# Where the loads of norm factors, the first weight casts and the token sums stand in a two-layer trunk kernel

## The chip, the core and the metric

The kernel runs on one core of a Trainium2 chip. The metric is the time of one execution on the device in microseconds (us); lower is better. The core has engines that run side by side: PE (TensorE, matrix products and transposes), DVE (VectorE), ACT (ScalarE), POOL (GpSimd) and SP (SyncE, which here issues every transfer from and to DRAM). Each engine takes its instructions strictly in the order in which they were laid down when the program was built; an instruction that waits holds up all that stands behind it on the same engine.

## The reference

Two layers work on `h` of 512 tokens by 1024 channels, all float32. Each layer has four stages, and each stage begins with an RMS norm of `h` ("pre") and ends with an RMS norm of what it made ("post"), which is added to `h`:

```
h = h + 0.5 * rmsnorm(swiglu(rmsnorm(h, g[0]), ffn1_gu, ffn1_down), g[1])
z = rmsnorm(h, g[2]) @ w_in
mixed = concat(hgrn2(z), window_attention(z), spatial_gating(z)) @ w_out
h = h + rmsnorm(mixed, g[3])
h = h + 0.5 * rmsnorm(swiglu(rmsnorm(h, g[4]), ffn2_gu, ffn2_down), g[5])
gate = sigmoid(rmsnorm(h, g[6]) @ ple_gate)
h = h + rmsnorm((p @ ple_proj) * gate, g[7])
```

`swiglu(x)` is `(silu(x @ W_gate) * (x @ W_up)) @ W_down` with 2816 inner channels. `g` are the norm factors, eight rows of 1024 per layer.

## The kernel before, in words

Every large product is made of three matmuls on pairs "hi" and "lo": hi is a value rounded to the format that PE reads (a cast on ACT), lo is the rest (a subtraction on DVE, `split_lo`, L137). Weights come by DMA into a ring of two float32 buffers (`wst`), are cast (L156, L151, L280) and split (L137), and only then may PE use them; a load waits until the split has freed its buffer. The first weights of a stage go into buffers of their own, `uwh` and `uwl`.

The 512 tokens are four tiles of 128. At the end of a stage each tile t goes through a chain. `post_tile` (L173): ACT squares the two halves of the accumulator (`tmp`, L178), DVE adds the sums (`v`, L180) and multiplies by the norm factors (`tmp`, L181), POOL makes the inverse root (`r`, L162), DVE updates `h` (L185, two halves). `pre_tile` (L200) does the same for the next stage: squares on ACT (L204), `v` (L206), `r`, and the normed tile `hn` on DVE (L209). Then a "turn": PE transposes `hn` (`ptr`, L215, two times four), ACT casts the result to the hi part of `hT` (L218) and DVE subtracts the lo part (L219).

An ffn stage works on gate and up columns in 11 blocks of 256 columns. The first block is plain (`gu`, L238). The other ten are products of 2 x 2 blocks by Strassen's scheme with seven products instead of eight (M1 to M7, banks X, Y, Z, L361). For these the weights come in four quarters b11, b21, b12, b22 (`wraw`, L311), and differences of them are made on DVE (L321), cast (L316) and split. M1 needs b11, M2 b21, M5 (bank Z) b12 - b11, M6 (bank X again) b22 - b12 + b11. On the side of the tokens it needs four sums and differences S1 to S4 of four 512 x 256 quarters of `hT`: `token_sums` first adds hi and lo of each quarter (`A`, L292; two quarters on POOL, two on DVE), then combines them (L296), casts and splits. The finished `g` goes out to DRAM (`gd`), is read back for the down product (`acc`), and is cast and split there.

The mix stage begins with products for the spatial gate (`sg`) and goes on with `zf`, its recurrences, attention and `wo`. Its constants are loaded in `mix_params`, called in the middle of the ffn before it; the last step there is a matrix `wT`: PE transposes it (L629) and DVE multiplies it by a triangle (L631). The ple stage begins with `gate` and `pj` products.

The stages are generators. The main loop (L1177 to L1190) runs stage i to its end, starts stage i+1 up to its first `yield` (its first weights), and then makes the chains of the four tiles. A scheduler orders what each engine does, within what it is told: `tc.keep_in_program_order` (the code's `pin`) keeps an instruction behind the one pinned before on the same engine, `tc.issue_after(x)` keeps what is made within it behind x. On SP each load stands in one queue. The loads of norm factors (`gain`, `load_gain`, L166) are made in `ends()`, ahead of the down product, but not pinned, and stood in the queue at the end of the stage, among the first weights of the next.

Of the kernel before, what the change touches and what calls it, by code (L numbers as in the profile page):

```python
# [2 lines left out]

# [1 line left out]

# [67 lines left out]
def kernel(ctx: ExitStack, tc: tile.TileContext, a: dict, out: bass.AP, phases=None):  # L73
# [59 lines left out]

    WST = 2

    def split_lo(out_, in_, hi, eng=nc.vector):
        eng.tensor_tensor(out=out_, in0=in_, in1=hi.bitcast(F32), op=ALU.subtract)  # L137

    def w_pair():
        return tuple(wpool.tile([P, 1024], F32R, tag=x, name=x) for x in ("whi", "wlo"))  # L140
# [1 line left out]
    def load_w(view, k=None, utag=None, eng=nc.vector):  # L142
        st = wpool.tile([P, 1024], F32, tag="wst", name="wst", bufs=WST)
        nc.sync.dma_start(st[:].rearrange("p (a b) -> p a b", a=k) if k else st[:], view)
        if utag and PHASE[cur["kind"]][utag][1] == 1024:
            hi, lo = ut("uwh", utag, F32R), ut("uwl", utag, F32R)
        elif utag:
            his = [ut("uwh", utag, F32R) for _ in range(2)]
            los = [ut("uwl", utag, F32R) for _ in range(2)]
            for n in range(2):  # L150
                nc.scalar.copy(his[n][:], st[:, n * 512:(n + 1) * 512])  # L151
# [4 lines left out]
        nc.scalar.copy(hi[:], st[:])  # L156
        split_lo(lo[:], st[:], hi[:], eng)
        return lambda c, w=512: (hi[:, c:c + w], lo[:, c:c + w])

# [6 lines left out]
    def load_gain(l, i):  # L166
        g = []
        for n in range(2):
            g.append(bpool.tile([P, 512], F32, tag="gain", name=f"gain{l}{i}{n}", bufs=4))
            nc.sync.dma_start(g[n][:], a["norm_gains"][l, i:i + 1, HN[n]].to_broadcast([P, 512]))  # L170
        return g

    def post_tile(t, parts, g, scale):  # L173
# [89 lines left out]
    def ffn(l, w_gu, w_down, i, ends, hook):  # L263
# [4 lines left out]
        def four(x):  # L268
            return x[:].rearrange("p (a b) -> p a b", a=4)
# [5 lines left out]
        for gu in range(2):  # L275
            for q in range(2):
# [4 lines left out]
                split_lo(lo[:], st[:], hi[:], nc.gpsimd if gu == q == 0 and i == 0 else nc.vector)  # L281
                w[gu, q] = hi, lo
        yield
        hT = hTs[i]
        turn(0)
        turn(1)

        def token_sums():
            def whole(half, q, tag, eng):
                x = ut("A32", "z") if tag == "z" else wpool.tile([P, 1024], F32, tag=tag, name="A32", bufs=WST)  # L290
                hi, lo = (hT[1][y][:, :, HALVES[half]].bitcast(F32) for y in (q, 2 + q))
                eng.tensor_tensor(out=four(x), in0=hi, in1=lo, op=ALU.add)  # L292
                return x

            def make(n, x, y, op, out):
                nc.vector.tensor_tensor(out=out[:], in0=x[:], in1=y[:], op=op)  # L296
                nc.scalar.copy(S[n][0][:], out[:])
                split_lo(S[n][1][:], out[:], S[n][0][:])

            a11, a12 = (whole(0, q, "z", nc.gpsimd) for q in range(2))  # L300
            a21, a22 = (whole(1, q, "wst", nc.vector) for q in range(2))
            make(1, a21, a22, ALU.add, a22)
            make(3, a11, a21, ALU.subtract, a21)
            make(2, a22, a11, ALU.subtract, a11)
            make(4, a12, a11, ALU.subtract, a12)


# [65 lines left out]
        def prefetch(n=1):  # L373
            for _ in range(n):
                x = next(ahead, None)
                if x:
                    queue.append(x)

        for tok in HALVES:
            for m in range(2):  # L380
                for gu in range(2):
# [101 lines left out]
    def ple(l, i, ends):  # L483
# [7 lines left out]
        for k in range(2):  # L491
# [147 lines left out]
    def mix_body(l, i_, ends, prms):  # L639
# [530 lines left out]
    pre(1, "pm")  # L1170
    run = phase(0)
    next(run)
    load_x(2)
# [40 lines left out]
```

## Time and profile before

| | us |
|---|---|
| median of 3 runs | 2044.76 (2043.82 to 2045.81) |
| the profiled execution, its own time | 2045.54 |
| its span in the profile | 2043.8 |
| PE busy | 1961.9 |
| DVE busy | 1405.4 |
| ACT busy | 926.7 |
| POOL busy | 135.2 |

Times in the profile count from the start of the span. A row of the timeline has start, duration, engine, line, operation, output and inputs, shape and count, and in brackets the idle time before it with what ended it. Rows of the view by windows have the window, its length, PE busy time (instructions), the clock granted to PE as a share of full speed, the share of DMA time and GB/s.

### The profile page before, as it was taken

The numbers are of one execution on the slowest core, as the hardware profiler recorded it, in microseconds if no ns is written. First come the engines' busy times: TensorE is split into PE (matmuls) and PEld (weight loads), VectorE is DVE, ScalarE is ACT, GpSimd is POOL, SyncE is SP. The second block draws the span as 40 slices with busy tenths as digits, with TensorE's granted clock in tenths as the row PEclk, the third lists the DMA queues.
The fourth block names the chain that finished last, engine by engine and source line by source line (L and its number), as shares of the span: only waits on it lengthen the run. The fifth ranks groups of instructions, "written<-read, shape, count | busy, mean of one in ns | idle before, by whom it ended". The sixth has DMA issues, their size and how long they took to land.

```text
span 2043.8 us, 31112 instructions
## 1 busy us (share of the span) xinstructions
PE 1961.9 (96%) x12524; PEld 1759.5 (86%) x12524; DVE 1405.4 (69%) x2054; ACT 926.7 (45%) x1467; POOL 135.2 (7%) x143
## 2 busy tenths in 40 slices
PE   6999999999989999998989999999999899999988
PEld 6999988788769999887789999887877799998866
DVE  7888663679769888434688785347798687874354
ACT  4544442554545445323454553335545455453242
POOL 2000000113110000000110000001130100000000
PEclk9999999999999999999999999999999999999999
DMA  6534263423225342542254433535141254335421
GB/s 195 175 120 140 85 206 120 147 60 116 77 67 168 115 147 84 177 146 90 72 170 126 149 112 111 176 114 151 56 129 42 73 165 155 109 99 185 144 95 50
DMA packets 160033, 251.18 MB, mean 123 GB/s; under 512 B 11408, under 2 KB 116752, under 8 KB 159888
## 3 DMA queue, kind: packets, MB, share of 16 engines
q1 hardware_dynamic: 159888, 249.19, 38.2%
q8 instruction: 98, 1.61, 0.3%
q14 instruction: 47, 0.39, 0.1%
HBM read 217.17 MB, written 29.36 MB: 121 GB/s over the span
## 4 chain that ended last, share of the span: by engine, by line
PE 79%; DVE 11%; DMA 4%; ACT 3%; issue 2%; POOL 1%; SPq 0%; DVEq 0%; POOLq 0%; ACTq 0%
PE X L361 22%; PE Z L361 11%; PE acc L235 8%; PE acc L234 8%; PE acc L233 8%; PE Y L361 5%; DVE wlo L137 2%; DMA wst<-in_ffn_gate_up_dram 2%; PE gate L234 1%; PE gate L235 1%; DMA wraw<-in_ffn_gate_up_dram 1%; PE gate L233 1%; PE gu L238 1%; DVE Pm L973 1%; DVE hn L209 1%
## 5 line engine op out<-in xcount | busy, mean ns | idle before, releaser
L316 ACT CAST whi<-wraw 128x1024 fp32r<-128x1024 f32 x280 | 291.9, 1050 | 363.1 <-DVE wraw L321 138.5
L137 DVE TENSOR_TENSOR wlo<-wraw,whi 128x1024 fp32r<-128x1024 f32 x280 | 340.4, 1221 | 101.1 <-ACT whi L316 100.3
L137 DVE TENSOR_TENSOR wlo<-wst,whi 128x1024 fp32r<-128x1024 f32 x148 | 185.2, 1251 | 153.6 <-ACT whi L156 152.5
L234 PE MATMUL acc<-wlo,gh 128*128 128x512 f32 x704 | 274.3, 390 | 0.1
L233 PE MATMUL acc<-whi,gh 128*128 128x512 f32 x704 | 274.2, 389 | 0.0
L235 PE MATMUL acc<-whi,gl 128*128 128x512 f32 x704 | 273.4, 390 | 0.0
L156 ACT CAST whi<-wst 128x1024 fp32r<-128x1024 f32 x140 | 147.1, 1051 | 206.2 <-PE acc L235 83.3
L361 PE MATMUL X<-hT,whi 128*128 128x256 f32 x1280 | 232.7, 283 | 3.1 <-DVE c L435 3.1
L321 DVE TENSOR_TENSOR wraw<-wraw 128x1024 f32<-128x1024 f32 x160 | 194.9, 1222 | 14.7 <-DMA wraw<-in_ffn_gate_up_dram 11.2
L361 PEld LDWEIGHTS X<-hT,whi 128*128 128x128 f32 x1280 | 199.6, 192 | 3.9 <-DVE c L435 3.9
L361 PE MATMUL X<-hT,wlo 128*128 128x256 f32 x640 | 181.1, 283 | 0.0
L235 PEld LDWEIGHTS acc<-whi,gl 128*128 128x128 f32 x704 | 132.1, 188 | 29.0 <-DVE gl L468 1.6
L234 PEld LDWEIGHTS acc<-wlo,gh 128*128 128x128 f32 x704 | 132.2, 188 | 28.5 <-DVE wlo L137 1.2
L233 PEld LDWEIGHTS acc<-whi,gh 128*128 128x128 f32 x704 | 132.2, 188 | 27.0
L162 POOL TENSOR_TENSOR r<-v,mhalf 128x1 f32<-128x1 f32 x64 | 38.1, 595 | 1715.4 <-DVE v L180 1608.6
L468 DVE TENSOR_TENSOR gl<-gl,gh 128x1024 fp32r<-128x1024 f32 x44 | 53.9, 1224 | 102.2 <-ACT gh L467 102.0
L361 PEld LDWEIGHTS X<-hT,wlo 128*128 128x128 f32 x640 | 122.8, 192 | 0.0
L361 PE MATMUL Y<-hT,whi 128*128 128x256 f32 x640 | 116.9, 283 | 0.0
L361 PEld LDWEIGHTS Y<-hT,whi 128*128 128x128 f32 x640 | 99.8, 192 | 0.0
L467 ACT CAST gh<-gl 128x1024 fp32r<-128x1024 f32 x44 | 46.3, 1053 | 110.4 <-PE acc L234 105.2
L361 PE MATMUL X<-S2h,wlo 128*128 128x256 f32 x320 | 91.5, 286 | 4.0 <-DVE wlo L137 4.0
L361 PE MATMUL X<-S2h,whi 128*128 128x256 f32 x320 | 91.2, 285 | 0.4 <-ACT whi L316 0.4
(326 smaller groups left out, 4694.9 us busy)
## 6 DMA issues: line engine op xcount, KB each, us to landing
wraw<-in_ffn_gate_up_dram SPq DMA_DIRECT2D x160, 512.0 KB, 5.4
wst<-in_ffn_down_dram SPq DMA_DIRECT2D x88, 512.0 KB, 3.4
gd<-g SPq DMA_DIRECT2D x44, 512.0 KB, 6.2
gl<-gd SPq DMA_DIRECT2D x44, 512.0 KB, 3.4
wst<-in_w_in_dram SPq DMA_DIRECT2D x36, 512.0 KB, 3.8
gain<-in_norm_gains_dram SPq DMA_DIRECT2D x32, 256.0 KB, 4.7
wst<-in_ffn_gate_up_dram SPq DMA_DIRECT2D x16, 512.0 KB, 6.5
wst<-in_w_out_dram SPq DMA_DIRECT2D x16, 512.0 KB, 3.4
```

The lines of the kernel that those rows point to most:

```text
L137: eng.tensor_tensor(out=out_, in0=in_, in1=hi.bitcast(F32), op=ALU.subtract)
L156: nc.scalar.copy(hi[:], st[:])
L162: nc.gpsimd.tensor_tensor(out=r, in0=v, in1=mhalf[:, :w], op=ALU.pow)
L209: nc.vector.scalar_tensor_tensor(out=hn[n][:], in0=h[t][n][:], scalar=r, in1=g[n][:], op0=ALU.mult, op1=ALU.mult)
L233: pin(nc.tensor.matmul(acc, lh, rh, start=first, stop=False))
L234: pin(nc.tensor.matmul(acc, lh, rl, start=False, stop=False))
L235: pin(nc.tensor.matmul(acc, ll, rh, start=False, stop=last))
L316: nc.scalar.copy(hi[:], x[:])
L321: nc.vector.tensor_tensor(out=out[:], in0=x[:], in1=y[:], op=ALU.subtract)
L361: pin(nc.tensor.matmul(acc[:, m * 256:(m + 1) * 256], x[:, c], y, start=fresh and m == k == n == 0, stop=m == 1 and k == 3 and n == 2, ski ...
L467: nc.scalar.copy(gh[:], gl[:].bitcast(F32))
L468: nc.vector.tensor_tensor(out=gl[:], in0=gl[:].bitcast(F32), in1=gh[:].bitcast(F32), op=ALU.subtract)
```

## The change

Three edits:

1. `load_gain` pins its DMAs, which puts the loads of norm factors on SP where the code stands: at the beginning of the down product, or behind the last loads of the output weights in mix, and no longer among the next stage's first weights.
2. `mix` and `ple` yield twice, each time with the newest hi cast and lo split. The main loop wraps the chain of tile 0 in `issue_after` of the first pair and its turn in that of the second. So the first weights of the stage (two of mix, four of ple) are cast and split ahead of tile 0's norms, and more of them ahead of tile 0's turn. The ffn yields twice with nothing, so there the wrapping is empty.
3. In `token_sums` all four sums of hi and lo are on DVE, pinned; the order is two sums, S1, one sum, S3, S2, one sum, S4. `prefetch(1)`, which loads b11 and b21 of the second block and casts the weight of M1, stands ahead of the token loop instead of within it.

```
 def load_gain(l, i):
-            nc.sync.dma_start(g[n][:], a["norm_gains"][l, i:i + 1, HN[n]].to_broadcast([P, 512]))
+            tc.keep_in_program_order(nc.sync.dma_start(g[n][:], a["norm_gains"][l, i:i + 1, HN[n]].to_broadcast([P, 512])))
...
+    @contextmanager
+    def behind(marks):
+        with ExitStack() as st:
+            for x in marks or ():
+                st.enter_context(tc.issue_after(x.ins))
+            yield
+
+    def marks():
+        return newest["hi"], newest["lo"]
...
 def token_sums():
-                eng.tensor_tensor(out=four(x), in0=hi, in1=lo, op=ALU.add)
+                pin(nc.vector.tensor_tensor(out=four(x), in0=hi, in1=lo, op=ALU.add))
...
-            a11, a12 = (whole(0, q, "z", nc.gpsimd) for q in range(2))
-            a21, a22 = (whole(1, q, "wst", nc.vector) for q in range(2))
+            a21, a22 = (whole(1, q, "wst") for q in range(2))
             make(1, a21, a22, ALU.add, a22)
+            a11 = whole(0, 0, "z")
             make(3, a11, a21, ALU.subtract, a21)
             make(2, a22, a11, ALU.subtract, a11)
+            a12 = whole(0, 1, "z")
             make(4, a12, a11, ALU.subtract, a12)
...
+        prefetch(1)
         for tok in HALVES:
...
-                prefetch(1)
                 token_sums()
                 prefetch(2)
...
 def ple(l, i, ends):
-        wg = [load_w(a["ple_gate"][l, k * P:(k + 1) * P, :], utag="bcc"[k] if k < 3 else None) for k in range(KD)]
-        yield
+        wg = []
+        for k in range(KD):
+            wg.append(load_w(a["ple_gate"][l, k * P:(k + 1) * P, :], utag="bcc"[k] if k < 3 else None))
+            if k in (1, 3):
+                yield marks()
...
 def mix_body(l, i_, ends, prms):
-        w = rows_cols(1792, 2)
-        yield
+        w = []
+        for j in range(4):
+            w.append(load_w(W[j * 256:(j + 1) * 256, 1792:].rearrange("(k p) c -> p k c", p=P), 2, "e" if j < 2 else None))
+            if j in (1, 2):
+                yield marks()
...
-            next(run)
+            ahead = next(run)
         for t, parts, g, scale, npre in todo:
-            post_tile(t, parts, g, scale)
-            turns[t] = npre(t, later=True)
+            with behind(ahead if t == 0 else None):
+                post_tile(t, parts, g, scale)
+                turns[t] = npre(t, later=True)
...
+            if t == todo[0][0] and i + 1 < len(seq):
+                ahead = next(run)
             if t < 2:
-                turn(t)
+                with behind(ahead if t == 0 else None):
+                    turn(t)
```

How the change moves instructions shows in three places. The first is DVE where the first ffn ends and mix begins, in layer 0. `tmp` and `h_80`, `h_81` are tile 0's post norm, `hn` its pre norm, `wT` the matrix of the spatial gate. Before:

```order
L181 SCALAR_TENSOR_TENSOR tmp_3628<-acc00_2766,gain010_2746 128x512
L631 TENSOR_TENSOR wT_3004<-wT_2999,triu_2997 128x512
L180 TENSOR_SCALAR v_3630<-ssq_3627 128x1
L181 SCALAR_TENSOR_TENSOR tmp_3629<-acc01_2767,gain011_2748 128x512
L185 SCALAR_TENSOR_TENSOR h_80<-tmp_3628,r_3636,h_80 128x512
L185 SCALAR_TENSOR_TENSOR h_81<-tmp_3629,r_3636,h_81 128x512
```

And now:

```order
L197 SCALAR_TENSOR_TENSOR tmp_3616<-acc00_2766,gain010_2746 128x512
L196 TENSOR_SCALAR v_3618<-ssq_3615 128x1
L197 SCALAR_TENSOR_TENSOR tmp_3617<-acc01_2767,gain011_2748 128x512
L201 SCALAR_TENSOR_TENSOR h_80<-tmp_3616,r_3624,h_80 128x512
L652 TENSOR_TENSOR wT_3004<-wT_2999,triu_2997 128x512
L201 SCALAR_TENSOR_TENSOR h_81<-tmp_3617,r_3624,h_81 128x512
L139 TENSOR_TENSOR wlo_3644<-wst_3641,whi_3643 128x1024
L222 TENSOR_SCALAR v_3635<-ss_3630 128x1
L225 SCALAR_TENSOR_TENSOR hn_3631<-h_80,r_3637,gain020_2750 128x512
L225 SCALAR_TENSOR_TENSOR hn_3632<-h_81,r_3637,gain021_2752 128x512
```

The multiplication of `wT` has moved from ahead of tile 0's update of `h` to between its two halves. On PE the four transposes that it waits for have moved too, from within the last accumulations to behind all of them.

The second place is ACT where the second ffn ends and ple begins, in layer 0: `uwh` are the first weights of ple, `tmp` the squares of tile 0's post norm, `hT30` the hi part of its transposed tile. Before:

```order
L156 CAST uwh_9172<-wst_9170 128x1024
L218 CAST hT30_8439<-ptr_9276 128x512
L156 CAST uwh_9178<-wst_9176 128x1024
L218 CAST hT30_8439<-ptr_9283 128x512
L178 ACTIVATE tmp_9292,ssq_9290<-acc11_8446 128x512
L156 CAST uwh_9206<-wst_9204 128x1024
```

And now:

```order
L142 CAST uwh_9172<-wst_9170 128x1024
L142 CAST uwh_9178<-wst_9176 128x1024
L142 CAST uwh_9206<-wst_9204 128x1024
L142 CAST uwh_9212<-wst_9210 128x1024
L194 ACTIVATE tmp_9217,ssq_9216<-acc00_8443 128x512
L194 ACTIVATE tmp_9218,ssq_9216<-acc01_8444 128x512
L142 CAST uwh_9242<-wst_9240 128x1024
L220 ACTIVATE hn_9230,ss_9229<-h_5194 128x512
L220 ACTIVATE hn_9231,ss_9229<-h_5195 128x512
L142 CAST whi_9248<-wst_9246 128x1024
```

Four casts have moved ahead of tile 0's squares, and two more ahead of its `hT`.

The third place is the queue of SP where the second ffn of layer 0 begins. `wst` are weights of the first block, `wraw_6066` is b12 of the second block and `wraw_6072` its b22, `wraw_6308` to `wraw_6374` are the quarters of the third block. Before:

```order
L278 DMA wst_5876<-in_ffn2_gate_up_dram 128x4x256
L278 DMA wst_5882<-in_ffn2_gate_up_dram 128x4x256
L311 DMA wraw_6066<-in_ffn2_gate_up_dram 128x4x256
L170 DMA gain051_8433<-in_norm_gains_dram 128x512
L170 DMA gain060_8435<-in_norm_gains_dram 128x512
L170 DMA gain061_8437<-in_norm_gains_dram 128x512
L311 DMA wraw_6308<-in_ffn2_gate_up_dram 128x4x256
L311 DMA wraw_6310<-in_ffn2_gate_up_dram 128x4x256
L311 DMA wraw_6343<-in_ffn2_gate_up_dram 128x4x256
L311 DMA wraw_6072<-in_ffn2_gate_up_dram 128x4x256
```

And now:

```order
L294 DMA wst_5876<-in_ffn2_gate_up_dram 128x4x256
L294 DMA wst_5882<-in_ffn2_gate_up_dram 128x4x256
L329 DMA wraw_6308<-in_ffn2_gate_up_dram 128x4x256
L329 DMA wraw_6310<-in_ffn2_gate_up_dram 128x4x256
L329 DMA wraw_6343<-in_ffn2_gate_up_dram 128x4x256
L329 DMA wraw_6374<-in_ffn2_gate_up_dram 128x4x256
L329 DMA wraw_6066<-in_ffn2_gate_up_dram 128x4x256
L416 DMA gd0_5912<-g_6045 128x1024
L329 DMA wraw_6072<-in_ffn2_gate_up_dram 128x4x256
```

The gain loads have left the queue here. b12 has moved from the first loads to behind the third block's four quarters, and b22 to behind the store of the first block's `g`.

More of the change, by code (lines that the diff above doesn't have):

```diff
@@ L1 @@
 import math
-from contextlib import ExitStack
+from contextlib import ExitStack, contextmanager
 import numpy as np
@@ L134, with cast_hi @@
     WST = 2
+    newest = {}
     def split_lo(out_, in_, hi, eng=nc.vector):
-        eng.tensor_tensor(out=out_, in0=in_, in1=hi.bitcast(F32), op=ALU.subtract)
+        newest["lo"] = eng.tensor_tensor(out=out_, in0=in_, in1=hi.bitcast(F32), op=ALU.subtract)
+    def cast_hi(out_, in_):
+        newest["hi"] = nc.scalar.copy(out_, in_)
+    @contextmanager
[6 more added lines that the diff above has]
+        return newest["hi"], newest["lo"]
     def w_pair():
@@ L150, in load_w @@
             for n in range(2):
-                nc.scalar.copy(his[n][:], st[:, n * 512:(n + 1) * 512])
+                cast_hi(his[n][:], st[:, n * 512:(n + 1) * 512])
                 split_lo(los[n][:], st[:, n * 512:(n + 1) * 512], his[n][:], eng)
@@ L155, in load_w @@
             hi, lo = w_pair()
-        nc.scalar.copy(hi[:], st[:])
+        cast_hi(hi[:], st[:])
         split_lo(lo[:], st[:], hi[:], eng)
@@ L283, in ffn @@
         yield
+        yield
         hT = hTs[i]
@@ L288, in token_sums, with whole @@
         def token_sums():
-            def whole(half, q, tag, eng):
+            def whole(half, q, tag):
                 x = ut("A32", "z") if tag == "z" else wpool.tile([P, 1024], F32, tag=tag, name="A32", bufs=WST)
                 hi, lo = (hT[1][y][:, :, HALVES[half]].bitcast(F32) for y in (q, 2 + q))
-                eng.tensor_tensor(out=four(x), in0=hi, in1=lo, op=ALU.add)
+                pin(nc.vector.tensor_tensor(out=four(x), in0=hi, in1=lo, op=ALU.add))
                 return x
@@ L1172 @@
     next(run)
+    next(run)
     load_x(2)
```

## The prediction

> **What bounds the kernel now.** The page's first part says that the matmul engine works nearly all the time:
>
> ```profile
> PE 1961.9 (96%) x12524; PEld 1759.5 (86%) x12524; DVE 1405.4 (69%) x2054; ACT 926.7 (45%) x1467; POOL 135.2 (7%) x143
> ```
>
> So the edit can win or lose only where PE stands still. The list of waits of PE (engine, line, what it waited for: us in total, times, longest) names the places:
>
> ```profile
> PE ptr L215 <- DVE hn L209: 32.0, 14, 7.8
> PE gate L233 <- ACT uwh L156: 6.4, 2, 3.2
> PE X L361 <- DVE wlo L137: 4.0, 3, 1.8
> PE gate L234 <- DVE uwl L137: 4.0, 2, 2.1
> ```
>
> `ptr` are the transposes of normed tokens, waiting for norms at a stage's end; `gate` waits for the first weights of ple; `X` for a split weight difference in an ffn. The counts of two are the two layers, and the edit reorders both layers alike, so I work the first out and count it twice.
>
> A wait costs more than itself. The view by windows (busy us of PE, granted clock) shows it on the chip's own 3.41 us grid:
>
> ```profile
> 384.39:387.80 3.41, 1.48 (x7) 1.00 0.80 219
> 387.80:391.21 3.41, 3.07 (x7) 0.50 0.82 275
> 585.78:589.19 3.41, 0.16 (x1) 1.00 0.00 0
> 589.19:592.60 3.41, 2.33 (x10) 0.50 0.00 0
> 592.60:596.02 3.42, 3.42 (x10) 0.50 0.00 0
> 957.83:961.24 3.41, 1.36 (x2) 0.50 0.40 154
> 961.24:964.66 3.42, 3.37 (x9) 0.50 0.47 153
> ```
>
> A window with PE busy for 1.48 or 0.16 us is followed by one at half clock, in which a full 3.41 us of work advances 1.7. So a wait of about 2 us costs 1.7 more, one of 4 us up to 3.4 more. [...]
>
> **Entry of mix (ffn1 to mix): a loss.** Before, the `wT` transposes stood early in the last accumulations and VectorE's multiplication of `wT` was done at 353.4; the norms of tile 0 followed and PE found them ready at 370.23:
>
> ```profile
> 353.38 0.69 DVE L631 TENSOR_TENSOR wT<-wT,triu 128x512 f32<-128x512 f32 x1 [0.75 <-PE wT L629]
> 355.67 1.42 DVE L185 SCALAR_TENSOR_TENSOR h<-tmp,r,h 128x512 f32<-128x512 f32 x2
> 358.82 1.41 DVE L209 SCALAR_TENSOR_TENSOR hn<-h,r,gain 128x512 f32<-128x512 f32 x2 [0.73 <-POOL r L162]
> 370.23 1.04 PE L215 MATMUL ptr<-ident,hn 128*128 128x128 f32 x8
> 388.14 0.80 PE L233 MATMUL sg<-uwh,hT 128*128 128x512 f32 x1 [2.28 <-ACT hT L218]
> 401.47 0.39 PE L233 MATMUL zf<-hT,whi 128*128 128x512 f32 x1
> ```
>
> Now `wT` is transposed behind the last accumulation, and its multiplication stands on VectorE between tile 0's two updates of `h`. So everything behind it (the second `h`, the squares, the norms of all four tiles) waits until about 370.2 (acc ends half of a 1.04 row earlier, four transposes follow). From there: the multiplication 0.7, then from the second `h` to the first `hn` as long as before, 356.4 to 359.5, about 3.2. With 0.2 of latency `ptr` starts near 374.4, a wait of 4.2. Behind it the norms of tiles 2 and 3, which used to be spread, come in a row on VectorE: I count 0.75 before the low half of tile 0, 0.8 in tile 1, and 2.4 around tile 2, whose low `hT` stands behind the updates of tile 3; 4.0 together. One half-clock window (1.7) follows. That is 9.9. Before, the same stretch lost 2.8 in waits, 2.28 of them the one that makes the window 384.39 idle, and 1.7 at half clock, 4.5. The casts moved ahead gain little here: before, PE began its `sg` matmuls 0.24 us after the transposes anyway. **+5.4 less 0.2 for cover of the half clock by those waits: +5.2.** Bounds: +3.5 (no half window), +8 (two, as after the wait at 590.27 below, and a longer tile 2).
>
> **Entry of ple (ffn2 to ple): a gain.** Before:
>
> ```profile
> 941.95 1.04 ACT L156 CAST uwh<-wst 128x1024 fp32r<-128x1024 f32 x1
> 954.88 1.05 ACT L156 CAST uwh<-wst 128x1024 fp32r<-128x1024 f32 x1
> 953.76 1.04 PE L215 MATMUL ptr<-ident,hn 128*128 128x128 f32 x8
> 957.99 1.36 PE L233 MATMUL gate<-uwh,hT 128*128 128x512 f32 x2 [3.19 <-ACT uwh L156]
> 961.24 0.80 PE L234 MATMUL gate<-uwl,hT 128*128 128x512 f32 x1 [1.89 <-DVE uwl L137]
> 983.80 0.63 PE L215 MATMUL ptr<-ident,hn 128*128 128x128 f32 x4 [0.37 <-DVE hn L209]
> ```
>
> ScalarE cast one weight at 941.95 and the next only at 954.88, behind a cast of `hT` that waited for PE's transposes, so 12 us of ScalarE went unused, and PE stood still for 3.19, 1.89, 0.42 and 0.37 (5.9) and ran the two windows from 957.83 at half clock (3.4). Now four weights are cast before tile 0's norms and two more before its `hT`. The norms come later (four casts and splits of 1.05 and 1.2 plus two loads in their way: 941.7 instead of 936), but are ready near 949, still ahead of 953.76: cover of 5 us. What is late next are the splits of the fifth and sixth weight, behind tile 1's updates: 0.7 and 0.75, with 0.7 of smaller waits, 2.2, and no window is idle for long. So 5.9 and 3.4 go and 2.2 comes: **−7.1.** Bounds −5 and −8.5.
>
> **Entry of ffn2 (mix to ffn2): a gain.** GpSimd sums tokens exactly while VectorE does the step that PE waits for:
>
> ```profile
> 587.30 3.48 DVE L209 SCALAR_TENSOR_TENSOR hn<-h,r,gain 128x512 f32<-128x512 f32 x2 [0.73 <-POOL r L162]
> 590.27 1.94 PE L215 MATMUL ptr<-ident,hn 128*128 128x128 f32 x8 [4.33 <-DVE hn L209]
> 603.28 3.45 POOL L292 TENSOR_TENSOR A<-hT,hT 128x1024 f32<-128x1024 f32 x1
> 604.39 3.55 DVE L185 SCALAR_TENSOR_TENSOR h<-tmp,r,h 128x512 f32<-128x512 f32 x2
> 610.48 0.66 PE L215 MATMUL ptr<-ident,hn 128*128 128x128 f32 x4 [2.16 <-DVE hn L209]
> ```
>
> Alone these steps take 1.41 and 1.42 (rows at 358.82 and 355.67); beside a sum 3.48 and 3.55. Without the sums the waits shrink by 2.07 and 2.06, one of the two half windows from 589.19 goes (1.7), and 0.4 for weights whose load no longer stands behind gain loads: **−6.2.** Bounds −4 and −8. The gain loads by themselves are worth that 0.4. At their new place, the start of the down product, they stand ahead of the third slice's weights, as three constant loads did in the first ffn:
>
> ```profile
> 249.43 0.40 PE L233 MATMUL acc<-whi,gh 128*128 128x512 f32 x1
> 249.66 0.40 PE L234 MATMUL acc<-wlo,gh 128*128 128x512 f32 x1
> 258.16 1.05 ACT L156 CAST whi<-wst 128x1024 fp32r<-128x1024 f32 x1 [6.25 <-DMA wst<-in_ffn_down_dram]
> ```
>
> The down product starts at 249.43 and takes 24 matmuls of 0.23 us a slice, so the third slice is due near 260.4: cover of 1 us behind its cast, and a cost of nothing while it holds; without it, four loads at 0.4 us of issue each, 1.6 per ffn.
>
> **Second block of every ffn (M5, M6): a loss.** The sums now cost VectorE two more 1.2 us steps, and the third weight quarter (b12) is loaded behind the four quarters of the next block, the fourth (b22) behind the store of `g`. Before:
>
> ```profile
> 625.20 4.82 SPq L311 DMA_DIRECT2D wraw<-in_ffn_gate_up_dram  x5
> 634.88 3.50 DVE L321 TENSOR_TENSOR wraw<-wraw 128x1024 f32<-128x1024 f32 x3 [2.61 <-DMA wraw<-in_ffn_gate_up_dram]
> 635.09 0.28 PE L361 MATMUL Z<-S1h,whi 128*128 128x256 f32 x1
> 639.56 0.38 PE L361 MATMUL X<-S2h,wlo 128*128 128x256 f32 x1 [1.20 <-DVE wlo L137]
> ```
>
> The five loads are freed by PE's reads, as now, so the fifth lands about when the fourth did here, 634.9. Then on VectorE: the difference b12−b11, S4's low part, c11, the low part of the difference: 1.2, 1.1, 0.6, 1.2, so M5 (`Z`) runs from 638.8 instead of 635.09. Its 24 matmuls take 3.0; b22's differences and split (two, a cast, a split) end at 643.6, where `X` went on at 639.56: +4.0, and 0.3 left of a half window that the second wait mostly covers. Per ffn: **ffn2 +4.3 in both layers; ffn1 of layer 0, which had no wait there, +4.2; ffn1 of layer 1, +3.2,** since it already lost 1.77 at half clock:
>
> ```profile
> 1067.60 0.58 PE L361 MATMUL X<-S2h,wlo 128*128 128x256 f32 x1 [1.77 <-DVE wlo L137]
> ```
>
> Bounds per ffn: +2 (b12 in the queue's shortest landing) to +7 (two half windows, later landing).
>
> **Entry of the two ffn1.** The same contention, smaller:
>
> ```profile
> 23.09 0.63 PE L215 MATMUL ptr<-ident,hn 128*128 128x128 f32 x4 [1.99 <-DVE hn L209]
> 27.07 0.63 PE L215 MATMUL ptr<-ident,hn 128*128 128x128 f32 x4 [2.04 <-DVE hn L209]
> 1037.87 0.52 PE L215 MATMUL ptr<-ident,hn 128*128 128x128 f32 x3 [2.58 <-DVE hn L209]
> ```
>
> In layer 0 4.0 of waits shrink to 1.3 (the fourth weight, landing at 23.7, is next): −2.7. In layer 1, 2.58 loses the 2.1 of a stretched step: −2.1.
>
> **Sum**, against the profiled execution's 2045.54 us: mix 2 × 5.2 = +10.4; ple 2 × −7.1 = −14.2; ffn2 entries 2 × −6.2 = −12.4; M5/M6 4.3 + 4.3 + 4.2 + 3.2 = +16.0; ffn1 entries −4.8. Total −5.0: 2040.5. The median of the runs shown is 0.8 below the profiled time, so 2040 as a median. About 0.2%, 4.1 us, is what a measurement of this kernel can tell from no change.
>
> **Rivals.**
> - *M5 and M6 cost 7 each (slower).* Place: the low part of b12's difference on VectorE, which waits for a load in the middle of a shared queue. If two windows at half clock follow instead of one partly covered (as at 589.19), or b12 lands 2 us later, each ffn loses 2.8 more: 4 × 2.8 = +11, 2052. It turns the total from 2.3 per ffn on. For it: the row at 589.19. Against: PE runs matmuls, not transposes, right behind the wait. Chance 0.20.
> - *Mix loses 8 each.* Two half windows behind a 4 us wait, as at 589.19 and 592.60; total −5.0 + 5.6, 2046. Chance 0.24.
> - *b12 is not late.* If its load lands at 632 and VectorE has slack before it, M5 and M6 lose 1 each: −17, 2028.5. For: 2.61 us of VectorE idle stood there. Against: the two sums fill that. Chance 0.13.
> - [...] Chance 0.05. [...]
>
> Forecast 0.38. That the edit does not do what it says is excluded by the order of instructions, which is fixed before the run. Faster by over 0.2%: 0.30 of the forecast (it lies near the bound), 0.13, 0.05, so 0.48; within: 0.08 and 0.20 of the mix case, 0.28; slower: 0.20 and 0.04, 0.24. The range 2028 to 2053 takes in the b12 case and the slow case.
>
> **What would show it.** Right: `ptr` behind a wait near 4 us at the entry of mix; no wait over 1 us in ple before its 48 gate matmuls of tile 1; `h` and `hn` at 1.4 everywhere and no GpSimd sum; `Z` of the second block behind a 3 to 4 us wait, then `X` behind one over 1. Wrong: no wait at `Z`, or the mix stage starting its `zf` at the same distance from the last `acc` as before, 31.2 us.

## The result and the profile after

| | before | after |
|---|---|---|
| median of 4 runs, us | 2044.29 (2043.15 to 2045.81) | 2056.25 (2055.23 to 2056.91) |
| profiled execution, its own time | 2045.54 | 2056.59 |
| its span | 2043.8 | 2054.8 |

The ratio is 1.0058, with a 95% interval from 1.004 to 1.0075: slower by 12 us, where 2040 had been forecast and 2053 was the end of the range. No work was added for PE. The page's first part of the changed kernel, and its list of waits of PE (engine, line, what it waited for: us in total, times, longest):

```profile
PE 1969.0 (96%) x12524; PEld 1765.8 (86%) x12524; DVE 1398.7 (68%) x2062; ACT 925.7 (45%) x1467; POOL 113.2 (6%) x135
```

```profile
PE ptr L231 <- DVE hn L225: 26.7, 14, 8.3
PE Z L379 <- ACT whi L334: 12.0, 4, 3.8
PE Z L379 <- DVE wlo L139: 7.7, 4, 4.2
PE acc L249 <- ACT whi L142: 4.7, 4, 1.4
```

The waits of `gate` have left the list, those of `ptr` are shorter, and two groups are new: `Z`, the first product that needs b12, four times twice, and `acc`, in the down products. To find where the time went I mark the start of each stage in both traces and compare the lengths of the stretches between them. The sum of the stretches is the difference of the spans (11.0) but for 0.4 before the first and behind the last mark.

| stretch, us after less before | forecast | ffn1, layer 0 / 1 | ffn2, layer 0 / 1 |
|---|---|---|---|
| entry of ffn1 (to the first X) | −2.7 / −2.1 | −2.1 / −1.6 | |
| entry of ffn2 (`wo` to the first X) | −6.2 each | | −4.1 / −7.3 |
| second block (first X to the third block's Y) | +4.2 / +3.2; +4.3 each | +8.4 / +4.4 | +5.8 / +5.9 |
| down product | 0 | +1.9 / +1.0 | +1.4 / +1.2 |
| entry of mix (behind ffn1) | +5.2 each | +5.8 / +4.7 | |
| ple (behind ffn2) | −7.1 each | | −7.2 / −7.6 |

Mix and ple came out as forecast, and the entries of the ffns within 2.1 in sum. The second blocks lost 24.5 instead of 16.0, and the down products 5.5 instead of nothing. Those 14.0 are all but 1.6 of the 15.6 between the forecast sum and the traces.

**Second block.** In layer 0's ffn2 (timeline of PE: start, us, engine, line, operation, and in brackets the idle time before it with what ended it):

```profile
644.90 0.28 PE L379 MATMUL Y<-hT,wlo 128*128 128x256 f32 x1
648.28 0.39 PE L379 MATMUL Z<-S1h,whi 128*128 128x256 f32 x1 [3.10 <-ACT whi L334]
650.07 0.58 PE L379 MATMUL Z<-S1h,wlo 128*128 128x256 f32 x1 [1.26 <-DVE wlo L139]
654.93 0.41 PE L379 MATMUL X<-S2h,whi 128*128 128x256 f32 x1
```

`Z` waits 4.4 in two pieces. Before, `X` waited 1.2, so the waits grew by 3.2, where 4.0 had been forecast for `Z` and `X` together. But `X`, which was to have the second wait, waits for nothing: from 650.07 to 654.93 PE works at a granted clock of 0.50 (rows of 0.41 where they took 0.28, and 0.21 us from the start of one to the next where it was 0.12). The view by windows on the clock's grid, for the half-clock windows of the second blocks of the four ffns (PE, weight loads, DVE, ACT, POOL busy, with counts; granted clock; share of DMA; GB/s):

```profile
54.70:58.11 3.41, 1.04 (x5) 1.04 (x6) 3.38 (x3) 0.00 (x0) 0.00 (x0) 0.50 0.08 25
58.11:61.53 3.42, 3.42 (x18) 3.42 (x18) 3.39 (x4) 2.94 (x3) 0.00 (x0) 0.50 0.00 0
648.59:652.00 3.41, 2.15 (x11) 1.93 (x10) 3.41 (x4) 0.63 (x1) 0.00 (x0) 0.51 0.48 154
652.00:655.42 3.42, 3.42 (x18) 3.42 (x18) 3.38 (x4) 3.05 (x4) 0.00 (x0) 0.50 0.00 0
...
sum 27.32, PE 21.66 PEld 21.15 DVE 27.15 ACT 13.93 POOL 0.00; mean PE 2.71 PEld 2.64 DVE 3.39 ACT 1.74 POOL 0.00
```

In the eight windows PE worked 21.66 us at half clock, by the granted 0.50 an estimated 10.8 lost; before, one window with 2.86 of work cost 1.4 there by the same count. So of the 24.5, about 9.4 is half clock; the waits of `Z` and `X` grew from 4.4 (no wait, 1.20, 2.18, 1.04 in the four ffns) to 19.7 (5.93, 4.36, 5.08, 4.34), 15.3.

**Down product.** ACT, PE and the queue of SP at the third slice of layer 0's ffn1, in this order:

```profile
266.80 1.04 ACT L142 CAST whi<-wst 128x1024 fp32r<-128x1024 f32 x1 [8.52 <-DMA wst<-in_ffn_down_dram]
```

```profile
267.90 1.43 PE L249 MATMUL acc<-whi,gh 128*128 128x512 f32 x5 [1.07 <-ACT whi L142]
```

```profile
257.73 2.23 SPq L186 DMA_DIRECT2D gain<-in_norm_gains_dram  x4
260.32 0.80 SPq L160 DMA_DIRECT2D wst<-in_ffn_down_dram  x2
```

Four gain loads go out from 257.73, and the third slice's weights only at 260.32. The cast waits for them until 266.80, and PE for the cast.

**Mix and ple.** Where `wT` is multiplied (DVE), and what PE waits for:

```profile
379.07 0.69 DVE L652 TENSOR_TENSOR wT<-wT,triu 128x512 f32<-128x512 f32 x1 [14.41 <-PE wT L650]
379.68 0.74 DVE L201 SCALAR_TENSOR_TENSOR h<-tmp,r,h 128x512 f32<-128x512 f32 x1
382.49 1.42 DVE L225 SCALAR_TENSOR_TENSOR hn<-h,r,gain 128x512 f32<-128x512 f32 x2 [0.73 <-POOL r L178]
```

```profile
383.30 1.97 PE L231 MATMUL ptr<-ident,hn 128*128 128x128 f32 x8 [4.27 <-DVE hn L225]
```

```profile
972.13 0.50 PE L249 MATMUL gate<-uwh,hT 128*128 128x512 f32 x1 [0.24 <-ACT hT L234]
977.35 0.51 PE L250 MATMUL gate<-wlo,hT 128*128 128x512 f32 x1 [0.35 <-DVE wlo L139]
```

DVE stands idle for 14.41 us in front of that multiplication, with the second update of `h` held behind it, whose `tmp` was done at 363.84 and `r` at 363.87, and PE then waits 4.27 at `ptr`: 4.2 had been forecast. In ple nothing is left above 0.5 before the first tile's gate.

**Entry of ffn2.** DVE and PE in layer 0: the step takes 1.42 instead of 3.48, and PE's wait behind it 2.28 instead of 4.33.

```profile
602.92 1.42 DVE L225 SCALAR_TENSOR_TENSOR hn<-h,r,gain 128x512 f32<-128x512 f32 x2 [0.73 <-POOL r L178]
```

```profile
603.82 1.69 PE L231 MATMUL ptr<-ident,hn 128*128 128x128 f32 x8 [2.28 <-DVE hn L225]
```

### The profile page after: what moved, and what is told of

The parts are those of the page before. It is cut to its first block, busy times and chain, and to the rows that moved or that the text cites. A ratio compares the mean times of both kernels' runs of the same rounds, so it can differ in the third digit from the quotient of the medians.

```text
span 2054.8 us, 31098 instructions
## 1 busy us (share of the span) xinstructions
PE 1969.0 (96%) x12524; PEld 1765.8 (86%) x12524; DVE 1398.7 (68%) x2062; ACT 925.7 (45%) x1467; POOL 113.2 (6%) x135
## 4 chain that ended last, share of the span: by engine, by line
PE 66%; DVE 8%; DMA 3%; ACT 2%; issue 1%; POOL 1%; SPq 0%; DVEq 0%; POOLq 0%; ACTq 0%
PE X L379 16%; PE Z L379 9%; PE acc L249 5%; PE acc L251 5%; PE acc L250 5%; PE Y L379 4%; PE gu L254 3%; DMA wraw<-in_ffn_gate_up_dram 1%; PE gate L251 1%; PE gate L249 1%; PE gate L250 1%; DMA wst<-in_ffn_down_dram 1%; PE wo L249 1%; PE ptr L231 1%; PE wo L251 1%
## 5 line engine op out<-in xcount | busy, mean ns | idle before, releaser
L379 PE MATMUL Z<-S1h,whi 128*128 128x256 f32 x320 | 95.0, 297 | 12.0 <-ACT whi L334 12.0
L379 PE MATMUL Z<-S1h,wlo 128*128 128x256 f32 x320 | 95.3, 298 | 7.7 <-DVE wlo L139 7.7
L379 PE MATMUL Z<-S1l,whi 128*128 128x256 f32 x320 | 94.4, 295 | 0.0
```

Source lines behind the costliest of these rows:

```text
L379: pin(nc.tensor.matmul(acc[:, m * 256:(m + 1) * 256], x[:, c], y, start=fresh and m == k == n == 0, stop=m == 1 and k == 3 and n == 2, ski ...
```

## The experiments

My theory was that the second blocks lose by late loads of b12 and b22 and by half clock behind them, the down products by the pinned gain loads, and mix by `wT`; the rivals are named with each run. Ratios are to the kernel before on the same chip (the changed kernel: 1.0058). Runs of one program spread over up to 13 us (2041.1 to 2054.3 in 31 runs of the kernel before), so where a few us matter I read the stretches of the trace. A stretch still holds the half-clock windows of its one trace, each worth up to 1.7 (3.41 at a clock of 0.50).

**1. The sums without the pin.**

```
-                pin(nc.vector.tensor_tensor(out=four(x), in0=hi, in1=lo, op=ALU.add))
+                nc.vector.tensor_tensor(out=four(x), in0=hi, in1=lo, op=ALU.add)
```

> The changed kernel with the four token sums still on VectorE but no longer pinned; nothing else differs. In the queue b12 of the second block then stands ahead of the third block's four quarters again. Theory A (the lateness of b12 is what costs, and the pin of the sums put it there): the waits of Z and X in the second blocks go to under 1.5 us each, the stretch from Y of the second block's ffn to the third block loses at most 2 per ffn instead of 8.4, 5.8, 4.4 and 5.9, and the time falls by 16 to 22, to 2034 to 2040. Rival B (the two more sums on VectorE cost that time, wherever b12 stands): Z still waits 3 us or more, and the time stays within 4 of 2056.

Measured: 2041.35, ratio 0.9976 [0.9962, 0.999], a little above the range of theory A; rival B is out. The second blocks take 23.9, 27.1, 26.7 and 27.0 (ffn1 and ffn2 of layer 0, then of layer 1), where the changed kernel took 31.4, 30.3, 31.4 and 30.2 and the one before 23.0, 24.5, 27.0 and 24.3. So 18.5 of the 24.5 are back, at one line. In this kernel DVE also made the four sums one behind the other, ahead of S1; what put the loads late was not settled by this run.

**2. The gain loads without the pin.**

```
-            tc.keep_in_program_order(nc.sync.dma_start(g[n][:], ...))
+            nc.sync.dma_start(g[n][:], ...)
```

> The changed kernel with the loads of norm factors not pinned, so that they stand again among the next stage's first weights. Theory A (the pinned loads delay the third and fourth slice's weights of each down product): the waits of acc of about 1 to 1.4 us at 266.8, 281.0, 860.2, 1286.4 and 1874.4 go, 5 us in all; 0.4 comes back at each entry of ffn2; 2050 to 2053. Rival B (those waits belong to the store and reload of g, or to the two constant loads in the same queue): they stay, and the time stays within 1.5 of 2056.

Measured: 2055.67, ratio 1.005 [1.0034, 1.0067], about the changed kernel's. Both halves of that are large. The down products win 2.3, 1.7, 1.7 and 1.3, 7.0 in all, so theory A holds there. But the first blocks of three ffns lose 4.6, 3.0 and 4.3, 11.9 (the fourth, in layer 0's ffn1, wins 1.1), where I had put 0.4 on an entry. PE in layer 0's ffn2:

```profile
621.21 1.87 PE L254 MATMUL gu<-hT,whi 128*128 128x256 f32 x8 [2.97 <-ACT whi L296]
```

PE waits here for weights of the first block, which stand behind gain loads in the queue. Before, a stretched norm held PE at nearly the same place; with that gone, the loads are what ends last.

**3. Mix without marks.**

```
             if j in (1, 2):
-                yield marks()
+                yield
```

> The changed kernel in which mix gives no marks, so that nothing of tile 0 is held behind its first casts; ple keeps its marks. Theory A (the marks are what moved the four transposes of wT behind the last accumulation, and the multiplication of wT into tile 0's norms): the multiplication stands ahead of tile 0's update of h again, ptr of mix waits under 1 us instead of 4.2, the two entries of mix cost 0 to 1 instead of 5.8 and 4.7; 2045 to 2047. Rival B (the loss at mix belongs to the pinned gain loads or to the down product ahead of it): ptr still waits 3 us or more and the time stays above 2052.

Measured: 2042.65, ratio 0.9982 [0.9966, 0.9997], below the expected 2045 to 2047; the profiled run, of 2046.54, is the slowest of the ten. From the end of ffn1's `acc` to the first `zf` it is 32.0 and 31.5 in the two layers; 36.9 and 36.2 in the changed kernel, 31.1 and 31.5 before. The multiplication of `wT` is early (DVE), and `ptr` follows `acc` without a wait (PE):

```profile
360.66 0.69 DVE L652 TENSOR_TENSOR wT<-wT,triu 128x512 f32<-128x512 f32 x1 [0.75 <-PE wT L650]
```

```profile
377.52 1.04 PE L231 MATMUL ptr<-ident,hn 128*128 128x128 f32 x8
```

So without the marks 9.6 of the 10.5 that mix had lost are back, and nothing else is lost there.

**4. Mix with marks, `wT` early.** The call of `hook()`, which makes the constants and `wT`, stands ahead of the accumulators instead of at the fifth slice.

```
+        hook()
         gpost, npre = ends()
...
-            if k == 4:
-                hook()
```

> The changed kernel with its marks in mix kept, but the constants and wT of mix made ahead of the down product's accumulators instead of in its fifth slice, so that wT's bank does not wait for an accumulator of tile 0 and its multiplication stands on VectorE near the first slices. Theory A (it is wT between the two updates of h that costs at mix): the wait of ptr falls from 4.2 to under 1.5 and the entry of mix costs between -1 and +2 instead of 5.8 and 4.7, so 2046 to 2050, if the constants' loads cost nothing at their new place. Rival B (the casts and splits ahead of tile 0's norms cost that time themselves): ptr still waits 3 us or more though wT is long done, and the time stays within 3 of 2056.

Measured: 2052.23, ratio 1.0024 [1.0007, 1.0041]. The stretch at mix is 30.6 and 31.8, about as before the change, though the casts stand ahead of tile 0's norms:

```profile
271.69 0.68 DVE L651 TENSOR_TENSOR wT<-wT,triu 128x512 f32<-128x512 f32 x1
```

```profile
381.37 1.03 PE L231 MATMUL ptr<-ident,hn 128*128 128x128 f32 x8
```

So it is `wT`, and the casts themselves cost nothing that shows. The time stayed above the expected 2046 to 2050. The first down product is 5.5 longer than in the changed kernel: the constants' loads now stand ahead of its weights in the queue, and PE waits 3.97 for a cast there and 1.53 for the multiplication of `wT`. The expectation had excepted that cost.

**5. The marks of ple alone, on the kernel before.** All of the change undone except the two `yield marks()` in ple and what the main loop needs for them.

> The kernel before with one part of the change alone: ple gives its marks, so that four of its first weights are cast ahead of tile 0's norms and two more ahead of its turn. Theory A (the marks alone gain at ple what the changed kernel gains there): the waits of 3.19, 1.89 and 0.42 go, the half-clock windows at 957.8 and 1971.6 go, each layer's ple starts 7 to 7.6 earlier, 2029 to 2032. Rival B (part of that gain belongs to the pinned gain loads, which left the queue ahead of ple's weights): each layer gains 3 to 5, 2034 to 2039.

Measured: 2030.82, ratio 0.9931 [0.9917, 0.9945], as theory A has it. Ple is 7.2 and 7.6 shorter, the same as in the whole change, and `gate` waits 0.24 instead of 3.19:

```profile
954.15 0.50 PE L249 MATMUL gate<-uwh,hT 128*128 128x512 f32 x1 [0.24 <-ACT hT L234]
```

**6. Two of the sums on GpSimd again.**

```
-            a11 = whole(0, 0, "z")
+            a11 = whole(0, 0, "z", nc.gpsimd)
...
-            a12 = whole(0, 1, "z")
+            a12 = whole(0, 1, "z", nc.gpsimd)
```

> The changed kernel with two of the four token sums on GpSimd again, where they stood before the change (those two not pinned), all else as changed. b12 then stands ahead of the third block's quarters. Theory A (the sums on GpSimd stretch VectorE's steps beside them, and b12's late place is what costs later): the steps of h and hn beside the sums take 3.4 to 3.5 us again, the entries of the two ffn2 lose about 4 each and of the two ffn1 2 each, but the second blocks win back 5 to 6 per ffn, as without the pin; 2044 to 2050. Rival B (the gain at the entries came from the moved gain loads and casts alone): the entries stay as in the changed kernel, and the time is 2034 to 2040.

Measured: 2055.02 (2049.65 to 2056.83 in 4 runs), ratio 1.0051 [1.0035, 1.0066]: above the expected 2044 to 2050. The profiled run, of 2049.65, is the lowest of the four, and against the changed kernel's trace it shows 6.9 less; so of the total I conclude nothing. Its stretches speak: the second blocks are at 23.2, 27.2, 26.1 and 27.1, and the entries of ffn2 lose 3.0 and 6.4 against the changed kernel. DVE beside a sum:

```profile
593.99 3.48 DVE L225 SCALAR_TENSOR_TENSOR hn<-h,r,gain 128x512 f32<-128x512 f32 x2 [0.73 <-POOL r L178]
610.97 3.55 DVE L201 SCALAR_TENSOR_TENSOR h<-tmp,r,h 128x512 f32<-128x512 f32 x2
```

These steps took 3.48 and 3.55 before the change too, with a GpSimd sum beside them, and take 1.42 in the changed kernel, which has no such sum, so theory A holds at the entries. What in the core stretches them is not shown. Runs 2 and 6 together, all else as changed: with the sums off GpSimd but the gain loads where they were, an entry of ffn2 changes by +0.4 and −3.1 against before; with the gain loads moved but two sums on GpSimd by −1.1 and −1.0; with both by −4.1 and −7.3. Each was hiding the other.

**7 and 8. The repairs together, and then the gain loads behind the last slice.** Run 7 is runs 1 and 3 in one. Run 8 adds:

```
-        gpost, npre = ends()
         ORD = {0: "pt", 1: "pg", 2: "pm", 3: "pm"}
...
+            if k == KF - 1:
+                gpost, npre = ends()
             gs[k] = tuple(...)
```

> The changed kernel with the token sums not pinned and without marks in mix: the two repairs together. Theory A (the two losses lie in different stages and add): 16 less for the sums and 10 to 14 less for mix, 2027 to 2033. Rival B (they share a cover, such as the place on the clock's grid): one of them gives under half of what it gave alone, 2035 to 2040.

> As the kernel with the token sums unpinned and mix not marked, and with each ffn's gain loads, still pinned, behind the last slice's load of its down product instead of ahead of the third slice's. Theory A (the pinned loads cost the down products 1.3 to 2.3 each and win at the entries): the waits of acc at the third slice go and nothing comes at the entries, 5 to 7 less than without this step, 2021 to 2027. Rival B (the loads now stand ahead of the next stage's first weights and give the gain at ple and mix back): within 2 of the kernel without this step.

Measured: 2030.04, ratio 0.9932 [0.9919, 0.9944], and 2025.31, ratio 0.9901 [0.9887, 0.9914]. By the ratios the two repairs give 1.26% together, and 0.82% and 0.76% alone: each keeps most of its gain, though they add a little less than in full, at the limit of what these runs can tell. Run 8 beats both kernels, the changed one by 1.6%. Its down products are 2.8, 1.2, 1.6 and 1.4 shorter than in run 7, 7.0 in all. The third slice waits 0.45 instead of 1.83 in layer 0's ffn1. Nothing comes at ple; mix is 1.5 and 0.2 longer:

```profile
259.17 0.50 PE L250 MATMUL acc<-wlo,gh 128*128 128x512 f32 x1 [0.45 <-DVE wlo L139]
```

**9. b12 first, the sums pinned.** To part the load from the order on DVE:

```
             b11, b21 = raw(0, 0), raw(0, 1)
+            b12 = raw(1, 0) if mp == 1 else None
             yield split(b11)
-            b12 = raw(1, 0)
+            b12 = b12 or raw(1, 0)
```

> The changed kernel with the token sums pinned as changed, and one edit: the load of b12 of the second block is asked for together with b11 and b21, so it stands ahead of the third block's quarters, as it did without the pin. This parts the place of the load from the order of VectorE. Theory A (the place of b12 in the queue costs most of what the second blocks lose): each ffn wins back 3 to 8 between its first X and the third block's Y, 16 to 19 in all, 2037 to 2042. Rival B (it is the pinned sums' order on VectorE, and the load's place only goes with it): under 1.5 per ffn, 2050 or more.

Measured: three runs of 2052.9 to 2057.6, and a fourth of 7580, which the ratio leaves out; median 2057.54, ratio 1.0052 [1.0032, 1.0072]. Theory A fell: the second blocks take 29.5, 30.7, 31.3 and 31.3. `Z` waits for nothing now, but `X` behind it waits in its place, 13.3 and 6.8 in all:

```profile
PE X L380 <- ACT whi L334: 13.3, 4, 3.6
PE X L380 <- DVE wlo L139: 6.8, 4, 1.8
```

DVE and the queue of SP in layer 0's ffn2:

```profile
639.64 1.23 DVE L139 TENSOR_TENSOR S4l<-A,S4h 128x1024 fp32r<-128x1024 f32 x1 [0.50 <-ACT S4h L314]
642.31 3.50 DVE L339 TENSOR_TENSOR wraw<-wraw 128x1024 f32<-128x1024 f32 x3 [1.44 <-DMA wraw<-in_ffn_gate_up_dram]
```

```profile
637.36 0.34 SPq L417 DMA_DIRECT2D gd<-g  x1
638.53 2.73 SPq L329 DMA_DIRECT2D wraw<-in_ffn_gate_up_dram  x2
```

DVE waits for b22, whose load goes out at 638.53, behind the store of `g`. So I made the store the suspect.

**10. b22's load ahead of the store as well.** As run 9, with that load and that store pinned in program order.

```
+                if mp == gu == q == 1:
+                    pin(i)
...
-        nc.sync.dma_start(gd[0][:], G[:])
+        pin(nc.sync.dma_start(gd[0][:], G[:]))
```

> The kernel with the sums pinned as changed and b12 asked for with b11 and b21, and one more edit: b22's load of the second block and the store of the first block's g are pinned in the order in which they are written, so the load stands ahead of the store. Theory A (with b12 early it is b22 that ends last: its load stood behind the store and landed 3 us too late): b22 lands 2.5 to 3 earlier after the first X, the waits of the second X fall from 2.7 to 3.6 to under 1.2, and each ffn wins 2.5 to 4.5 between its first X and the third block's Y; 2041 to 2048. Rival B (the sums' late place on VectorE holds the subtractions of b22 whatever its load does): the waits stay over 2, and the time stays within 4 of 2057.

Measured: 2056.15, ratio 1.0054 [1.0035, 1.0073], as rival B has it; second blocks 28.8, 31.1, 31.2 and 31.4. The store was innocent. DVE and the queue:

```profile
637.78 1.22 DVE L313 TENSOR_TENSOR A<-A,A 128x1024 f32<-128x1024 f32 x1
643.21 3.50 DVE L341 TENSOR_TENSOR wraw<-wraw 128x1024 f32<-128x1024 f32 x3 [1.81 <-DMA wraw<-in_ffn_gate_up_dram]
```

```profile
628.82 10.61 SPq L329 DMA_DIRECT2D wraw<-in_ffn_gate_up_dram  x5
639.49 0.50 SPq L419 DMA_DIRECT2D gd<-g  x1
```

The fifth load, b22, is issued at 639.07, at the end of the L313 step at 637.78. That step is S4's combination, a12 less the buffer of a11, in which S2 stands by then. b22 gets that buffer: the ring has five, and b11, b21, b12 and the two sums fill it. The change put a12 behind S1 to S3, so S4 comes last, a11's buffer is read last, and b22 cannot be loaded until then. In the changed kernel it is the same: the step ends at 644.31, and b22's load goes out at 644.37 (DVE and the queue):

```profile
643.09 1.22 DVE L313 TENSOR_TENSOR A<-A,A 128x1024 f32<-128x1024 f32 x1
```

```profile
644.37 4.31 SPq L329 DMA_DIRECT2D wraw<-in_ffn_gate_up_dram  x2
```

In all fourteen traces, in each of the four ffns, a quarter's load goes out 0.03 to 0.08 us behind the later of the buffer's last two readers, the split of S2 and the combination of S4.

**11. The four sums first, pinned.** If that is so, the order of the sums is enough:

```
+            a11, a12 = (whole(0, q, "z") for q in range(2))
             make(1, a21, a22, ALU.add, a22)
-            a11 = whole(0, 0, "z")
             make(3, a11, a21, ALU.subtract, a21)
             make(2, a22, a11, ALU.subtract, a11)
-            a12 = whole(0, 1, "z")
```

> The changed kernel with the four token sums on VectorE and pinned, but written one behind the other ahead of S1 to S4, as they were before the change, instead of between them; nothing else differs. b12 then stands ahead of the third block's quarters and b22 among them. Theory A (it is the place of the sums between S1 to S4, which keeps buffers and with them the loads of b12 and b22 late, and not the pin as such): as without the pins, 16 to 20 less than the changed kernel, 2037 to 2042. Rival B (any pin of the sums costs): under 6 less, 2051 or more.

Measured: 2039.58, ratio 0.9972 [0.9959, 0.9985], as theory A has it; second blocks 24.2, 27.3, 28.3 and 27.3. S4's combination stands right at the first X (628.69); in the changed kernel it stands 3.8 us behind it, in run 10 4.8. The last reader of a11's buffer is now the split of S2, and b22's load goes out behind it, 2.4 behind the first X, instead of 5.1 and 6.1. `Z` waits 0.29. DVE and PE:

```profile
628.73 1.22 DVE L313 TENSOR_TENSOR A<-A,A 128x1024 f32<-128x1024 f32 x1
629.87 1.22 DVE L139 TENSOR_TENSOR S2l<-A,S2h 128x1024 fp32r<-128x1024 f32 x1
635.61 3.49 DVE L338 TENSOR_TENSOR wraw<-wraw 128x1024 f32<-128x1024 f32 x3
```

```profile
635.14 0.38 PE L378 MATMUL Z<-S1h,wlo 128*128 128x256 f32 x1 [0.29 <-DVE wlo L139]
640.28 0.39 PE L378 MATMUL X<-S2h,wlo 128*128 128x256 f32 x1 [1.77 <-DVE wlo L139]
```

So it is neither the pin as such (run 11 keeps it) nor the sums' being on DVE, nor the written order alone (run 1 keeps that), but a pin that holds the sums spread between S1 to S4.

**12. Run 8 with b12 first.** The edit of run 9 on the kernel of run 8.

> The kernel with sums unpinned, mix not marked and gain loads behind the last slice, and b12 asked for together with b11 and b21. Theory A (b12 is early enough there already, since Z of the second blocks waits for nothing): within 2 of the kernel without this step, 2023 to 2027. Rival B (the wait of X of 1.77 that is left in three of the four ffns hangs on the chain that begins with b12): that wait falls under 1, 1 to 2 per ffn, 2018 to 2022.

Measured: 2023.91, ratio 0.9898 [0.9879, 0.9916], the same as run 8 within the intervals. The waits of `X` stay at up to 1.8: rival B is out, and b12 was early enough. One second block, in layer 0's ffn2, is 3.6 longer than in run 8, 3.0 of it at half clock.

## Why the prediction was wrong

- **Entry of mix, +5.2 each: right** (+5.8 and +4.7), for the reason given: `wT` between tile 0's two updates of `h` (runs 3 and 4). The first wait is 4.27 where 4.2 was forecast. The 0.2 of latency in that sum no run shows: `ptr` starts at 383.30, 0.06 behind the end of the first `hn`. The rest is partly luck: in layer 0 the waits behind it are 2.4 instead of 4.0, and half clock costs 1.4 more than before, where no change was counted.
- **Ple, −7.1 each: right** (−7.2 and −7.6), by the marks alone (run 5). Two terms were off against each other: the windows at 957.83 and 961.24 hold 1.36 and 3.37 us of work, so half clock cost 2.4 there and not 3.4, and 1.1 of waits is left in layer 0 where 2.2 was forecast.
- **Entries of the ffns, −17.2: nearly right in sum** (−15.1), wrong in the shares. I put 0.4 of each ffn2 entry on the gain loads. Unpinned, they cost 4.6 and 4.3 there (run 2), since behind the stretched norms the first block's weights were next late by almost as much. Layer 0 got less than layer 1 by half clock: the waits fell by 5.5 and 4.6, but half clock cost 1.9 more in layer 0 (its windows at 546.2 are new) and 3.4 less in layer 1. In run 11, with waits 5.2 and 5.0 lower, it is the other way round: 2.9 less and 1.4 more.
- **Second blocks, +16.0: the step that failed is "+4.0, and 0.3 left of a half window that the second wait mostly covers".** The waits were sized well in sum, 15.3 against about 15, though not one by one: they grew by 5.9, 3.2, 2.9 and 3.3 (ffn1 and ffn2 of layer 0, then of layer 1). But the two waits came together ahead of and inside `Z`, none came at `X`, and PE had its two windows at half clock full of work: 9.4 where I allowed about 1. In layer 0's ffn1 the order that I took from ffn2 did not hold either. DVE takes up b22's difference ahead of the low half that `Z` needs, and waits 2.82 for its load:

```profile
54.65 1.23 DVE L339 TENSOR_TENSOR wraw<-wraw 128x1024 f32<-128x1024 f32 x1 [2.82 <-DMA wraw<-in_ffn_gate_up_dram]
55.80 1.22 DVE L139 TENSOR_TENSOR wlo<-wraw,whi 128x1024 fp32r<-128x1024 f32 x1
```

  So it lost 8.4 instead of 4.2. The rival "M5 and M6 cost 7 each" had this mechanism, two windows at half clock, and 2052; it measured 6.1 each. What was held against it, that PE runs matmuls and not transposes behind the wait, did not keep the second window away.
- **Down products, priced at nothing: failed by the named cover.** The text put it at 1 us and the loss without it at 1.6 per ffn. The cover did not hold in any of the four, and they lost 1.0 to 1.9.
- **The cause behind the second block** was read only half. The forecast saw b12 behind the third block's quarters, which is so, but run 9 shows that b12's place alone moves the wait from `Z` to `X`. What holds b22 is the place of the sums in a ring of five buffers (runs 10 and 11). For b12 the runs show only that it goes back ahead of the third block's quarters when the sums do; by which rule the scheduler put it behind is not shown.
- **The chance of 0.05** was given to a case that no run shows: windows with 1.48 us of work (before, 384.39) and 2.41 (after, 542.80) were followed by half clock.

What stays open: the second blocks of runs 1 and 11 still take 6 to 8 us more in sum than before the change, 2.4 and 3.6 of it in waits and the rest at half clock. `prefetch(1)` stands elsewhere there, and I did not undo that alone.

## What to carry to other kernels

When a helper's steps are put in another order, follow each buffer they read to the transfer that gets it next; the late transfer may be one that nobody moved. Price a new wait with the half-clock windows that follow it, unless the order shows another wait inside those windows, and look at each repetition's own order. Two delays that hide each other must be taken away together: here each was worth 1 to 1.5 on average alone, and 5.7 both.

## What the runs showed of the hardware

The window before the first half-clock window of layer 0's ffn2 held 0.31 us of work; in the changed kernel a full-clock window that half clock followed held up to 2.41 us of work (542.80 to 546.22), over the fourteen profiles of this case up to 2.47:

```profile
645.18:648.59 3.41, 0.31 (x2) 0.30 (x2) 2.67 (x3) 1.31 (x2) 0.00 (x0) 1.00 0.60 193
```

On the way out, before the change one half-clock window held 2.86 us of work, and full clock followed; after it one held 2.76, and half clock went on. These are the two rows, before and after:

```profile
1067.05:1070.46 3.41, 2.86 (x13) 2.86 (x14) 3.41 (x5) 3.03 (x5) 0.00 (x0) 0.50 0.48 154
1070.46:1073.88 3.42, 3.42 (x31) 3.42 (x30) 3.31 (x3) 1.53 (x2) 0.00 (x0) 1.00 1.00 293
```

```profile
1075.26:1078.67 3.41, 2.76 (x13) 2.76 (x14) 3.38 (x4) 0.58 (x2) 0.00 (x0) 0.50 0.50 152
1078.67:1082.09 3.42, 3.42 (x18) 3.42 (x18) 3.42 (x4) 3.42 (x5) 0.00 (x0) 0.50 0.08 11
```

In the profiles before and after, the 20 half-clock windows that full clock followed held 2.86 us of work or more, and the 12 that half clock followed 2.79 or less. Over the fourteen profiles of this case, the 130 half-clock windows that full clock followed held 2.86 us of work or more, and 40 of the 42 that half clock followed held 2.79 or less (the other two 3.01 and 3.41). So in these runs a half-clock window that a wait left nearly a fifth empty mostly cost a second one.

What such a window costs: in the same two profiles a matmul of 128x256 starts 213 ns behind the one before it at a clock of 0.50 and 120 ns at 1.00, one of 128x512 427 and 227 ns. So a window full of work loses 1.5 to 1.6 us of its 3.41, and the 1.7 and the halves counted above are a little high.

In both profiles every change of the granted clock lies on one grid of 3.41 us, and half clock lasts one or two windows of it (3.41 or 6.83 us) but for the last, which stands to the end of the records. Against the start of the span the grid stands 2.09 us behind a multiple of its step before and 0.09 after. One program's runs differ by up to 9 us in run 3 (2037.5 to 2046.5 in 10 runs); where each of them stood on the grid, and whether that makes the difference, is not shown.
